# Loading w by sets of rows and x's first chunks by channel halves, with eight output slots started side by side

## The chip, the cores and the metric

The kernel runs on one core of one Trainium2 chip. The metric is the device time in microseconds (us). Three runs of the kernel before gave a median of 903.98 us (903.84 to 904.01).

## The reference

A batch of sequences is multiplied by a square matrix, and the product is summed along the sequence with one decay for each output channel:

```python
B, S, D = (16, 2048, 1024)
xw = x @ w
out[:, 0, :] = xw[:, 0, :]
for t in range(1, S):
    out[:, t, :] = decay[None, :] * out[:, t - 1, :] + xw[:, t, :]
```

All of x (128 MB), w (4 MB) and the output (128 MB) are float32. The kernel multiplies in bf16 and accumulates in float32.

## The kernel before

**Chunks and slots.** The 32,768 rows of x are cut into 64 chunks of 512 rows (`TL`), four to a sequence, and the chunks are taken in pairs, `groups`. The 1024 output channels are eight slots `n` of 128 channels, made of 32 from each quarter of the channels. A step of the main loop is one slot of one pair of chunks, so a tile has 128 partitions (channels) and 1024 columns (time); the last two chunks are handled singly. The product of a slot and a chunk takes eight matrix products `k` (`K` = 8), each with 128 input channels and 512 columns, summed in one PSUM bank.

**From x to a product.** `load` (letter L, or M for the first two chunks) brings a chunk from DRAM to `xb` in four DMAs, one for each 32 partitions, on GpSimd's queue, casting to bf16 on the way. `turn` (letters T and E, line 115) transposes blocks of 32 by 32 on VectorE. It treats two bf16 channels as one 32-bit word, so that `xw` holds two neighbouring channels beside each other. `part` (letters X, Y, F, G, line 123) copies `xw` to `xt` and pulls the two channels apart. `matmul` (line 131) reads its columns either from `xt`, where they stand close, or from `xw` with a gap between them (`pairs`).

**w.** It is loaded once by `load_w` into the tiles that later hold outputs (`stage`), in four sets (h, e): h is the half of the columns, e the parity of the rows. The first set goes by SP's and ACT's queues as float32, the other three by GpSimd's queue (letter U) with a cast. `settle` (letters W, w, q, Q; lines 330 and 379) copies a set into `wsb` in the order that the products need.

**From a product to the output.** A tile is scanned along time on VectorE in one of two ways. A tile that isn't `paired` is scanned straight from PSUM (letter S, line 233). For a paired tile ACT copies the bank to `xs` (p, line 186) and scales the even columns (g, line 169), GpSimd joins them into the odd columns (j, line 208), VectorE scans half as many columns with the squared decay (S, line 213), and ACT and GpSimd fill the even columns in again (h, line 169, and c, line 266). `keep` (k, z) carries the last column to the next tile of the slot. VectorE transposes the result back (B, line 283) and SP stores it. A set `flips` of step numbers says which tiles take the other way than the rule by slot.

**PSUM.** There are eight banks: three double tiles `ps`, in turn, and two single ones, `spare` and `spare1`. A bank can be written again when ACT or VectorE has read it. `spare1` also holds the squared decays from the letter d on.

**The order of work.** Each engine works through its own instructions in the order in which the program writes them. This order is written out by hand for the start and the end, in `agenda`: a string of letters for each step, performed after the step's products have been written; step -99 stands for all before the first product. In between it follows a rule (`usual`), into which the turns and copies of later chunks are put by `later`. At most eight of GpSimd's DMAs are under way; the ninth is issued when the first has landed.

**The start.** TensorE first multiplies zeros (`spin`), and then goes on with gate tiles, one for each quarter of the first load (`spin_on`, letter K), so that these products wait for the load. Step 0 then works on four slots in two parts: the first chunk by halves of its rows, the even `k` first, in four banks; then the second chunk in four other banks. Steps 4 to 7 follow with two banks each, and step 8 interleaves two slots of the second pair of chunks.

Of the kernel before, what the change touches and what calls it, by code (L numbers as in the profile page):

```python
# [9 lines left out]
FP32 = mybir.dt.float32  # L10
# [15 lines left out]
def kernel(  # L26
# [82 lines left out]

    def turn(c, j0=0, j1=NJ, m0=0, m1=M):  # L110
        if c not in xw_of:
            xw_of[c] = ring(sb, "xw", 2, [128, M, NJ, P, 2], BF16)
        src = xb_of[c][:, j0:j1].rearrange("p j c -> p (j c)").bitcast(FP32)
        dst = xw_of[c].rearrange("p m j i e -> p (m j i e)").bitcast(FP32)
        pin(nc.vector.transpose(  # L115
            out=dst.rearrange("p (m j i) -> p j m i", m=M, i=P)[:, j0:j1, m0:m1],
            in_=src.rearrange("p (j m c) -> p j m c", m=M, c=P)[:, :, m0:m1]))
# [172 lines left out]
    class Outlet:  # L290
# [8 lines left out]
        def store(self, b, t0, j0, j1):  # L299
# [4 lines left out]
            for j in range(j0, j1, nj):  # L304
# [10 lines left out]
    size = M * CH  # L315
    stage = {(0, 0): room[0][:, 0:size],
             (0, 1): room[0][:, size:size * 3 // 2].bitcast(BF16),
             (1, 0): room[1][:, 0:size // 2].bitcast(BF16),
             (1, 1): room[1][:, size // 2:size].bitcast(BF16)}

    def load_w(queues, h, e):
        for i, q in enumerate((0, 2, 1, 3)):
            pin(queues[i % len(queues)].dma_start(  # L323
                out=stage[h, e][quad(q)].rearrange("p (m d) -> p m d", m=M),
                in_=_ap(w, [[2 * D, P], [2 * P * D, M], [1, CH]],
                        (q * CQ + e) * D + h * CH)))

    def settle(h, e, m, copy):
        src = stage[h, e][:, m * CH:(m + 1) * CH]
# [7 lines left out]
    load_w((nc.sync, nc.scalar), 0, 0)  # L337
# [21 lines left out]
    def load_half(i):  # L359
        for q in range(NQ):  # L360
            load(i // 2, q, *halves[i % 2])

    def spin_on(q):
        pin(nc.scalar.copy(out=gates[q][quad(q), 0:1], in_=xb_of[0][quad(q), 0, 0:1]))
        spin(3 if q < NQ - 1 else 2, gates[q])

    def load_part(i):
        load_w((nc.gpsimd,), *((0, 1), (1, 0), (1, 1))[i])
# [3 lines left out]

    def settle_one(i, copy):
        settle(i // 8, i // 4 % 2, i % 4, copy)

    def settle_slots(i, r0, r1):
        h, e, m = i // 8, i // 4 % 2, i % 4
        src = stage[h, e][:, m * CH:(m + 1) * CH]
        pin(nc.vector.tensor_copy(  # L379
            out=wcols[:, 2 * m + e, h, :, r0:r1],  # L380
            in_=src.rearrange("p (q r i) -> p q r i", q=NQ, r=R)[:, :, r0:r1]))
# [91 lines left out]
    slots = [(g, n) for g in groups[:-1] for n in range(K)]  # L473
# [3 lines left out]
    def turn_and_load(c):  # L477
# [15 lines left out]
        "W": lambda i: settle_one(i, nc.vector.tensor_copy),  # L493
        "w": lambda i: settle_one(i, nc.scalar.copy),
        "M": load_half,
        "U": load_part,
# [4 lines left out]
        "q": lambda i: settle_slots(i, 0, 1),  # L501
        "Q": lambda i: settle_slots(i, 1, R),
# [22 lines left out]
        -99: "M0 M1 U0 M2 M3 U1 U2 w0 W1 w2 W3 K0 K1 K2 K3 E0 E1 G0 E2 G1 E3 F2 G3 E4 E5 G4 E6 G5 E7 F6 G7 q4 w5 Q4 W6 W7 D E8 E9 G8 E10 G9 E11 F10 G11 E12 L E13 G12 L E14 G13 E15 L F14 G15",  # L525
        0: "p0 z0 W8 W9 W10 W11",
        1: "g0",
        2: "L S1 L",
        3: "p2 z2 L g2 j0 S3 w12 w13 L w14 L w15 k1",
        4: "j2 B1 d k3",  # L530
        5: "p4 L S0 L g4 S2 L k0 h0 j4 B3 h2",
        6: "k2 c0 T2 c2 p5 g5 B0 L X2 L",
        7: "B2 L L Y2 T3 L z4 z5 j5 p6 S4 z6 L g6 L X3 S5 j6 S7 Y3 L S6 h4 k7 k5 c4 k4 h5 B7",
        8: "",
        9: "k6 h6 c5 B4",
        10: "p8 g8 c6 T4 z8 p9 j8 g9 B5 X4",
        11: "L j9 B6 p10 S8 L z9 z10 g10 S9 h8",
        12: "j10 Y4 S11 L c8 h9 T5 c9",
        13: "p12 L g12 B9 j12 X5 S10 L",
        14: "Y5 B8 L B11 h10 z12 c10 S13",  # L540
        15: "p14 L g14 S12 j14 T6 h12 L",
# [186 lines left out]
```

## Time and profile before

| | |
|---|---|
| median of three runs | 903.98 us |
| profiled execution, its own device time | 903.68 us |
| its span, from first to last instruction | 901.9 us |
| TensorE busy | 892.0 us (99%) |
| VectorE, ACT, GpSimd busy | 825.6, 687.6, 657.0 us |
| granted TensorE clock | 1.00 throughout |
| read from and written to DRAM | 138.4 and 134.2 MB |

The span is one execution; 1.8 us of its device time lie outside it. A busy share is an average over the whole span. Products are pipelined: a product's length in the table (0.38 us) is longer than the time from one start to the next, so the pace is read from starts. An instruction's line is that of the helper that wrote it, and an engine's idle time in square brackets names what ended it.

### The profile page before, as it was taken

Reading aid. Unit: us, or ns where it says so; the run is one execution under the profiler, and the core shown is the slowest. Engines: PE = TensorE matmul, PEld = TensorE weight load, DVE = VectorE, ACT = ScalarE, POOL = GpSimd, SP = SyncE. Lnnn points to the kernel's source line nnn. Section 1 sums busy time; section 2 is a strip of 40 time slices with the busy share of each in tenths; the row PEclk is TensorE's granted clock in tenths of the full one; section 3 lists DMA queues with packets and bytes.
Section 4 is the critical chain, followed back from the end, with each engine's and each line's share of the span. In section 5 each row is a group of like instructions: output and inputs, shape, how many; then the busy total and the mean of one; then the engine's idle time right before and its main releaser. Section 6 shows DMA issues by size and latency. Waiting matters only on the chain.

```text
span 901.9 us, 12226 instructions
## 1 busy us (share of the span) xinstructions
PE 892.0 (99%) x4127; PEld 412.1 (46%) x4209; DVE 825.6 (92%) x636; ACT 687.6 (76%) x962; POOL 657.0 (73%) x755
## 2 busy tenths in 40 slices
PE   9999999999999999999999999999999999999998
PEld 5544444444444444444444444444444444444444
DVE  4999999999999999999998999999999999999998
ACT  4889867777877877878778778777787787787743
POOL 7888678777767768777677687777777777776532
PEclk9999999999999999999999999999999999999999
DMA  9999999999999999999999999999999999999768
GB/s 193 196 215 217 231 218 217 215 240 253 254 249 252 248 249 252 242 247 230 225 234 228 224 228 228 233 228 228 232 229 228 227 230 225 228 226 222 176 152 234
DMA packets 403182, 204.77 MB, mean 227 GB/s; under 512 B 9392, under 2 KB 402096, under 8 KB 403120
## 3 DMA queue, kind: packets, MB, share of 16 engines
q1 hardware_dynamic: 265808, 134.77, 60.9%
q0 software_dynamic: 137024, 68.70, 56.7%
q8 instruction: 33, 0.54, 0.2%
q10 hardware_dynamic: 288, 0.52, 0.2%
q14 instruction: 29, 0.24, 0.1%
HBM read 138.42 MB, written 134.22 MB: 302 GB/s over the span
## 4 chain that ended last, share of the span: by engine, by line
PE 97%; DMA 1%; issue 1%; POOL 0%; DVE 0%; ACT 0%; DVEq 0%; POOLq 0%
PE ps L131 96%; PE spare L131 1%; DMA xb<-in_x_dram 1%; DMA ot<-in_w_dram 1%; POOL ot L323 0%; DVE so L233 0%; PE ps L419 0%; PE spare L419 0%; ACT xb L426 0%; DVE wsb L379 0%; DVEq L379 0%; POOLq L712 0%
## 5 line engine op out<-in xcount | busy, mean ns | idle before, releaser
L131 PE MATMUL ps<-xt,wsb 128*128 128x512 bf16 x3934 | 860.8, 378 | 4.7 <-DVE wsb L379 0.4
L131 PEld LDWEIGHTS <-wsb 128*128 128x128 bf16 x4160 | 406.8, 98 | 478.7 <-ACT wsb L330 0.8
L208 POOL TENSOR_TENSOR xs<-h,xs 128x512 f32<-128x512 f32 (+1 forms) x190 | 243.0, 1279 | 189.8 <-ACT h L169 84.6
L186 ACT COPY xs<-ps 128x1024 f32<-128x1024 f32 (+1 forms) x190 | 188.9, 994 | 156.9 <-PE ps L131 146.3
L283 DVE STREAM_TRANSPOSE ot<-so 128x1024 f32<-128x1024 f32 (+2 forms) x265 | 300.4, 1172 | 2.5 <-POOL so L202 1.1
L266 POOL TENSOR_TENSOR so<-h,xs 128x512 f32<-128x512 f32 (+1 forms) x190 | 241.5, 1273 | 41.2 <-ACT h L169 27.0
L123 ACT COPY xt<-xw 128x2048 bf16<-128x2048 bf16 (+1 forms) x136 | 242.3, 1790 | 7.6 <-DVE xw L115 7.4
L105 POOL DMA_DIRECT2D xb<-in_x_dram x264 | 174.3, 661 | 3.0 <-POOLq L712 0.9
L169 ACT ACTIVATE h<-so,dec 128x512 f32<-128x512 f32 (+1 forms) x190 | 145.4, 766 | 25.5 <-DVE so L213 22.3
L115 DVE STREAM_TRANSPOSE xw<-xb 128x2048 f32<-128x2048 f32 (+1 forms) x78 | 147.3, 1900 | 5.3 <-DMA xb<-in_x_dram 5.3
L213 DVE TENSOR_TENSOR_SCAN so<-spare,keep,xs 128x512 f32<-128x512 f32 (+1 forms) x97 | 120.0, 1240 | 27.6 <-POOL xs L208 27.2
L213 DVE TENSOR_TENSOR_SCAN so<-spare,xs 128x512 f32<-128x512 f32 x93 | 113.3, 1220 | 27.2 <-POOL xs L208 24.4
L169 ACT ACTIVATE h<-ps,dec 128x512 f32<-128x512 f32 (+1 forms) x189 | 129.5, 685 | 0.0
L233 DVE TENSOR_TENSOR_SCAN so<-dec,ps 128x1024 f32<-128x1024 f32 x34 | 76.9, 2261 | 0.8 <-ACT h L169 0.6
L233 DVE TENSOR_TENSOR_SCAN so<-dec,keep,ps 128x1024 f32<-128x1024 f32 (+2 forms) x35 | 74.8, 2140 | 0.0
L270 ACT COPY keep<-so 128x1 f32<-128x1 f32 x136 | 25.4, 189 | 9.1 <-DVE so L233 8.6
L204 ACT COPY so<-keep 128x1 f32<-128x1 f32 x97 | 18.4, 191 | 2.4 <-DVE ot L283 2.2
L131 PE MATMUL spare<-xt,wsb 128*128 128x512 bf16 (+1 forms) x64 | 12.9, 332 | 0.0
L131 PE MATMUL ps<-xw,wsb 128*128 128x256 bf16 (+1 forms) x68 | 11.2, 301 | 0.0
L202 POOL MEMSET so<- 128x1 f32 x93 | 10.7, 117 | 0.6 <-DVE ot L283 0.6
L323 POOL DMA_DIRECT2D ot<-in_w_dram x12 | 6.5, 546 | 3.2 <-DMA xb<-in_x_dram 1.9
L348 PE MATMUL spare<-idle 128*128 128x512 bf16 x22 | 6.8, 483 | 1.2 <-DVE idle L338 1.2
(40 smaller groups left out, 40.5 us busy)
## 6 DMA issues: line engine op xcount, KB each, us to landing
out_dram<-ot SPq DMA_DIRECT2D x236, 512.0 KB, 10.8
xb<-in_x_dram POOLq DMA_DIRECT2D x248, 256.0 KB, 7.8
out_dram<-ot SPq DMA_DIRECT2D x56, 128.0 KB, 2.6
xb<-in_x_dram POOLq DMA_DIRECT2D x16, 128.0 KB, 5.7
out_dram<-ot SPq DMA_DIRECT2D x8, 256.0 KB, 4.5
ot<-in_w_dram POOLq DMA_DIRECT2D x12, 128.0 KB, 5.1
out_dram<-xb SPq DMA_DIRECT2D x4, 256.0 KB
ot<-in_w_dram ACTq DMA_DIRECT2D x2, 256.0 KB, 5.1
```

The source lines that it names most:

```text
L105: pin(nc.gpsimd.dma_start(out=xb_of[c][quad(q), j0:j1], in_=_ap(x, [[D, P], [P * D, j1 - j0], [1, CQ]], (b * S + t0 + j0 * P) * D + q * CQ)))
L115: pin(nc.vector.transpose(out=dst.rearrange("p (m j i) -> p j m i", m=M, i=P)[:, j0:j1, m0:m1], in_=src.rearrange("p (j m c) -> p j m c", ...
L123: pin(copy(out=xt_of[c][:, m0:m1, :, j0 * P:j1 * P], in_=src))
L131: pin(nc.tensor.matmul(out=ps[:, t0:t1] if ps.shape[1] >= t1 else ps, lhsT=lhs, rhs=rhs, start=(k == 0 and t0 == start), stop=(k == K - 1),))
L169: pin(nc.scalar.activation(out=h, in_=src, func=mybir.ActivationFunctionType.Copy, scale=dec[:, self.n:self.n + 1]))
L186: pin(nc.scalar.copy(out=self.xs[:, i * size:(i + 1) * size], in_=ps))
L208: pin(nc.gpsimd.tensor_tensor(out=odds, in0=self.g, in1=odds, op=ALU.add))
L213: pin(nc.vector.tensor_tensor_scan(out=so[:, 3:T + 2:2], data0=squares[-1][:, n:n + 1].to_broadcast([128, T // 2]), data1=self.xs[:, 1:T:2 ...
L233: pin(nc.vector.tensor_tensor_scan(out=so[:, t + 2:t + 2 + size], data0=dec[:, n:n + 1].to_broadcast([128, size]), data1=ps, initial=befor ...
L266: pin(nc.gpsimd.tensor_tensor(out=self.so[:, 2:T + 2:2], in0=self.h, in1=self.xs[:, 0:T:2], op=ALU.add))
L270: pin(nc.scalar.copy(out=self.keep, in_=self.so[:, self.T + 1:self.T + 2]))
L283: pin(nc.vector.transpose(out=outlet.ot[:, j:j + size, c0:c0 + P], in_=self.so[:, t1:t1 + size * P].rearrange("p (i t) -> p i t", t=P)))
```

## The change

Only the start is changed, up to step 41 of the new numbering.

- The first pair of chunks is no longer taken together: chunk 0 and chunk 1 are sixteen steps of 512 columns each, and later steps have numbers higher by eight.
- w comes in four sets `m` of 256 rows with all 1024 columns (64 rows from each quarter of the channels, each two neighbouring ones on one partition), so that a DMA moves 32 pieces of 8 KB instead of 128 pieces of 2 KB. Set m serves the products k = 2m and 2m + 1 of all eight slots.
- Chunks 0 and 1 are loaded by `load_side` in halves of channels (128 of each quarter's 256): five loads M0 to M4, of which M0, M3 and M4 are half a chunk and M1 and M2 a quarter. A piece is 512 B in DRAM and 256 B as written. `turn` has a branch for this layout.
- The queue on GpSimd becomes M0 U1 M1 U2 M2 U3 M3 M4.
- Step 0 writes the products of all eight slots for chunk 0 into all eight banks, in the order of k. The products k = 0, 1, 4, 5 are taken by halves of the rows and read `xw`; the others read `xt`.
- Chunk 1's products all read `xw`. Its first four slots (step 8) run side by side, then come four more, each to its end.
- The gate spins are 3, 2, 2 and 1 instead of 3, 3, 3 and 2.
- The agenda and the flips for the first 41 steps are new.

The diff, cut to its core:

```diff
+    def load_side(c, q, side, j0, j1):
+        ...
+        wide = CQ // 2
+        dst = xb_of[c].rearrange("p j c -> p (j c)").rearrange(
+            "p (g j c) -> p g j c", g=2, c=wide)
+        pin(nc.gpsimd.dma_start(
+            out=dst[quad(q), side, j0:j1],
+            in_=_ap(x, [[D, P], [P * D, j1 - j0], [1, wide]],
+                    (b * S + t0 + j0 * P) * D + q * CQ + side * wide)))
...
-                out=stage[h, e][quad(q)].rearrange("p (m d) -> p m d", m=M),
-                in_=_ap(w, [[2 * D, P], [2 * P * D, M], [1, CH]],
-                        (q * CQ + e) * D + h * CH)))
+                out=stage[m][quad(q)],
+                in_=_ap(w, [[2 * D, P], [1, 2 * D]], (q * CQ + 2 * m * P) * D)))
...
     def load_half(i):
+        c, side, j0, j1 = ((0, 0, 0, NJ), (0, 1, 0, H), (0, 1, H, NJ),
+                           (1, 0, 0, NJ), (1, 1, 0, NJ))[i]
         for q in range(NQ):
-            load(i // 2, q, *halves[i % 2])
+            load_side(c, q, side, j0, j1)
...
-        spin(3 if q < NQ - 1 else 2, gates[q])
+        spin((3, 2, 2, 1)[q], gates[q])
...
-    slots = [(g, n) for g in groups[:-1] for n in range(K)]
+    slots = [([c], n) for c in groups[0] for n in range(K)]
+    slots += [(g, n) for g in groups[1:-1] for n in range(K)]
...
-        -99: "M0 M1 U0 M2 M3 U1 U2 w0 W1 w2 W3 K0 K1 K2 K3 E0 E1 G0 E2 G1 E3 F2 G3 E4 E5 G4 E6 G5 E7 F6 G7 q4 w5 Q4 W6 W7 D E8 E9 G8 E10 G9 E11 F10 G11 E12 L E13 G12 L E14 G13 E15 L F14 G15",
+        -99: "M0 U1 M1 U2 M2 U3 M3 M4 w1 W0 w3 W2 K0 K1 K2 K3 E0 E4 E1 E5 G1 G5 W4 W5 W6 w7 E2 E3 G3 D W8 W9 W10 w11 E6 E7 G7 W12 W13 W14 w15",
+        7: "z3 z2 L S1 L L p3 E12 k1 p2 L S0 g3 L g2 p4 E8 j2 E9 k0 E13 S2 E15 E10 E14 j3 S3 E11",
+        11: "g4 j4 k2 h2 L c2 k3 h3 B0 L p5 B1 c3 g5 S4 j5 p6 B3 k4 z4 g6 z5 L S5 h4 j6 B2 k5 h5 T2 c4",
+        13: "z6 c5 p7 g7 z7 L p10 j7 S6 X2 B5 L S7 L S9",
+        14: "g10 L k6 h7 j10 h6 B4 k9 c7 Y2 B9",
+        15: "c6 S8 L p11 L S13 T3 p14 g11 g14",
...
-    flips = (1, 13, 15, -19, -18, -11, -8, -6, -3, -2)
+    flips = (0, 1, 3, 7, 8, 9, 11, 12, 13, 16, 19, 21, 23, 27, 35, 37, 38, -19, -18, -11, -8, -6, -3, -2)
...
+            both = [ring(psp, "ps", 3, [128, 2 * TL]) for _ in range(3)]
+            heads = [ps[:, i * TL:(i + 1) * TL] for ps in both for i in range(2)] + spares
             for k0 in range(0, K, 2):
+                if k0 in (0, M):
+                    for j0, j1 in halves:
+                        for k in (k0, k0 + 1):
+                            for i in range(K):
+                                matmul(heads[i], i, k, xt_of.get(0), j0 * P, j1 * P,
+                                       pairs=xw_of[0])
+                elif k0 < M:
+                    for k in (k0, k0 + 1):
+                        for i in range(K):
+                            matmul(heads[i], i, k, xt_of[0])
+                else:
+                    for i in range(K):
+                        for k in (k0, k0 + 1):
+                            matmul(heads[i], i, k, xt_of[0])
...
+        elif step == K:
+            both = [ring(psp, "ps", 3, [128, 2 * TL]) for _ in range(2)]
+            ...
+            for i0 in range(0, R, 2):
+                for k in range(M):
+                    for i in range(i0, i0 + 2):
+                        matmul(heads[i], i, k, xt_of.get(1), pairs=xw_of[1])
             for i in range(R):
+                for k in range(M, K):
+                    matmul(heads[i], i, k, xt_of.get(1), pairs=xw_of[1])
```

## The prediction

> **What bounds the kernel now.** I read the page's busy lines first, then what TensorE waited for, then the timelines of TensorE and VectorE over the first 50 us, where the change lies.
>
> The page's busy line and TensorE's waits over the whole span:
>
> ```profile
> PE 892.0 (99%) x4127; PEld 412.1 (46%) x4209; DVE 825.6 (92%) x636; ACT 687.6 (76%) x962; POOL 657.0 (73%) x755
> ...
> PE spare L348 <- DVE idle L338: 1.2, 1, 1.2
> PE spare L348 <- ACT gate L364: 0.4, 1, 0.4
> PE ps L131 <- DVE wsb L379: 0.4, 1, 0.4
> ```
>
> TensorE is the bound, and it waits for almost nothing. Whatever the change does reaches the end only through the start of the first real product, the pace of a product, and new waits of TensorE. Its timeline (start, length, operation):
>
> ```profile
> 8.45 2.55 PE L348 MATMUL spare<-idle,gate 128*128 128x512 bf16 x11 [0.44 <-ACT gate L364]
> 10.83 0.50 PE L131 MATMUL ps<-xw,wsb 128*128 128x256 bf16 x3
> ...
> 15.04 0.82 PE L131 MATMUL ps<-xt,wsb 128*128 128x512 bf16 x2 [0.36 <-DVE wsb L379]
> ...
> 41.20 1.89 PE L131 MATMUL spare<-xt,wsb 128*128 128x512 bf16 x8
> 42.93 3.79 PE L131 MATMUL ps<-xw,wsb 128*128 128x512 bf16 x16
> 46.55 3.61 PE L131 MATMUL ps<-xt,wsb 128*128 128x512 bf16 x15
> ```
>
> Real work starts at 10.83, right behind the eleven gate spins. Eight products from xt take 42.93 - 41.20 = 1.73 us, so 0.216 each; sixteen from xw, whose rows are read with a gap, take 46.55 - 42.93 = 3.62 us, so 0.226. A 256-wide product from xw takes 0.113 (10.83 to 12.53: 15 starts in 1.70). The sixteen xt products before 42.93 are slot 8's first, so chunks 0 and 1 end at 42.93 - 16 x 0.216 = 39.48. That is the mark to beat: with everything behind it unchanged, the change is worth its shift of this mark.
>
> VectorE's timeline shows when the load sets arrive, as each first instruction waits for one:
>
> ```profile
> 9.58 1.42 DVE L115 STREAM_TRANSPOSE xw<-xb 128x256 f32<-128x256 f32 x4 [1.62 <-DMA xb<-in_x_dram]
> 12.21 1.43 DVE L115 STREAM_TRANSPOSE xw<-xb 128x256 f32<-128x256 f32 x4 [0.89 <-DMA xb<-in_x_dram]
> 14.79 0.36 DVE L379 COPY wsb<-ot 128x128 bf16<-128x128 bf16 x2 [0.85 <-DMA ot<-in_w_dram]
> 17.53 1.42 DVE L115 STREAM_TRANSPOSE xw<-xb 128x256 f32<-128x256 f32 x4 [1.35 <-DMA xb<-in_x_dram]
> 20.23 1.42 DVE L115 STREAM_TRANSPOSE xw<-xb 128x256 f32<-128x256 f32 x4 [0.96 <-DMA xb<-in_x_dram]
> ...
> 26.76 1.19 DVE L233 TENSOR_TENSOR_SCAN so<-dec,spare 128x512 f32<-128x512 f32 x1
> ```
>
> The loads arrive in a stream without gaps: M0 at 9.58, M1 at 12.21, U0 at 14.79, M2 at 17.53, M3 at 20.23. An x set (four DMAs, 1024 packets of 512 B, 0.5 MB as written) takes 2.63, 2.74, 2.70, mean 2.69 us; the w set (512 packets of 1 KB, as many bytes) 2.58. The two rows give a price: 0.11 us for 512 packets more, and 2.47 us for the bytes.
>
> **The change, part by part.**
>
> *Loads.* The order on POOL's queue becomes M0 U1 M1 U2 M2 U3 M3 M4. A row of x is cut in two, so a set M0, M3 or M4 has 2048 packets of 256 B: 2.47 + 4 x 0.11 = 2.91 us. M1 and M2 are half sets of 1024: 1.46. A w set has 128 packets of 4 KB: 2.50. No row shows x packets under 512 B. The lower bound is the price by bytes alone (2.69); the upper is a packet that costs as much as one of 512 B (5.38, and 2.69 for M1, M2). I take 2.91, on the line through the two rows and near the lower end, because halving the packets there changed the time by only 4%. What waits for a set can then start: M0 9.58 + 0.22 = 9.80, U1 12.30, M1 13.76, U2 16.26, M2 17.72, U3 20.22, M3 23.13, M4 26.04. POOL issues a 512-packet DMA in 0.66 us against the 0.73 that it moves in, and eight DMAs may be under way, so issuing keeps ahead; M1 and M2 issue at 0.58 each against 0.36, but their turn to issue comes when M0 lands (about 8 us) and they move from 12.3 on. The first w set on SP and ACT has longer rows; I cost that at nothing, as the casts that need it (7.16 and 7.20) have over 2 us until M0.
>
> The Trainium skill (DMA: Bandwidth & Descriptors, Specifications) says that line rate needs transfers of at least 512 B and that below it the engine does a read-modify-write. That speaks against this change; no trace here shows it, and by it the time would be that of the first rival below.
>
> *First product.* The gates keep the spins until M0's last quarter has landed; there are 8 instead of 11. Gate copy (0.19) after 9.76, one spin (0.22), the turn of the first tile 9.80 + 0.36: the first product starts at 10.25 instead of 10.83. Gain 0.6.
>
> *Slots 0 to 7 of chunk 0, in eight banks.* Channels 0-1 by halves: 32 x 0.113 = 3.63, to 13.88. Channels 2-3: U1 at 12.30 and three copies of 0.29 are done by 13.2, so 16 x 0.216 = 3.45 runs at once, to 17.33. Channels 4-5: U2 16.26, its first copy 16.6 and third 17.15; M2's first turn 18.1, needed at 19.14; 3.63, to 20.96. Channels 6-7: U3 20.22, copies at 20.5, 20.8 and 21.1; the third is needed at 21.18; 3.45, to 24.41. No wait, but the last margin is 0.1.
>
> *The step to chunk 1.* Its first product needs the turns E8 and E12 and the bank pair ps0, which scans S1 and S0 empty; VectorE's order is S1, E12, S0, E8. Slot 1 ends at 20.96 + 3 x 0.216 + 0.38 = 22.0. S1 (1.19, the row above) ends at 23.2, just when M3 is there (23.13); E12 0.36, S0 1.15, E8 0.36: 25.1. TensorE would have come at 24.41, so here is a new wait of 0.7. Queued behind E8 are the turns E9 and E13, which products 0.45 us later need and get.
>
> *Chunk 1's 64 products* read xw: 64 x 0.226 = 14.5 against 13.8 from xt. That costs 0.7. The 256-wide xw products stay 64; 32 from xt (0.109 each) go, worth 0.04. The two waits of before in this stretch (0.36, and about 0.2 not listed but seen as gaps in starts) go.
>
> Sum: 25.15 + 14.5 = 39.65 against 39.48, so +0.2.
>
> *What is late next.* Slot 16 needs ps0 again, emptied by S9 and S8. VectorE's order from E8 on, by row means (256 transposes 0.36, half scans 0.73, 512 turns back 0.62 as half of 1.22, T2 2.27, 512 scans 1.2): E9 E13 S2 E15 E10 E14 S3 E11, 28.7; B1 B0 S4 B3 S5 B2, 32.7; T2, 34.9; S6 B5 S7 S9 B4 B9, 39.4; S8, 40.6. Back to back, each starts some 0.07 earlier than the row before ends (24.57 + 2.27 against 26.76), which takes 1.5 off: 39.1. Slot 16 wants it at 39.65. So a wait of 0 to 0.9; I take 0.3. T3 for chunk 3 (by 42.5 to 44) is wanted at 43.1 plus that wait: nothing.
>
> *Load on the engines.* Eight whole tiles become sixteen half ones. By counts and row means: VectorE 16 transposes of 0.68 for 8 of 1.22, 9 half scans of 0.73 and net 5 of 1.25 for 5 of 1.25 and 2 of 2.3, fewer copies: +2 us. ACT -2, POOL +0.3. VectorE works without a gap from 25 to 110 us (10.00 of 10.00 in the stretch 100 to 110) and has 16.52 of 20.00 after 120. The 2 us are thus absorbed there, if the banks come free in time meanwhile; cost 0, upper bound 2. The end part is as it was.
>
> Total: -0.6 + 0.7 + 0.7 - 0.6 (waits gone) + 0.3 = +0.5 us. On the profiled run (901.9 span, 1.8 outside it, 903.68) that is 904.2; the median is 0.3 higher, so 904.5.
>
> **Rivals.**
>
> 1. *Small packets cost more.* If a 256-B packet took as long as one of 512 B, the sets come at M0 12.3, U1 14.8, M1 17.5, U2 20.0, M2 22.7, U3 25.2, M3 30.6, M4 35.9; E12, S0 and E8 let chunk 1 start at 32.5, it stops at 36.1 until M4's turns at 37.0 and ends at 37.0 + 48 x 0.226 = 47.9: +8.4, 912.4. Halfway (4.03 a set) M3 comes at 26.5, chunk 1 starts at 28.5 and ends at 43.0: +3.5, 907.5. It decides from a set price of about 3.5, where M3 is 1.5 us late and S0 and E8 still stand behind it. For: no row. Against: the small effect from 1 KB to 512 B. Chance 0.19, most of it nearer the half.
>
> 2. *VectorE's queue gives the banks back late.* S0 before E8, S8 at slot 16, T3, and the margin of 0.1 at U3 all sit on one engine that is full until 110 us. If the row means held without overlap (0.9 at slot 16) and the 2 us of added work showed as bank waits before 110, it is +0.2 + 0.9 + 1 to 2: 906.1 to 907.1. For: the 10.00s. Against: before lives with the same fullness and TensorE waits for none of it. Chance 0.17.
>
> 3. *The head start is larger.* If w's long rows free the engines sooner and M0 lands 0.7 earlier, everything up to S1 moves: first product 9.5, chunk 1 at 24.4: -0.5, 903.5; with no wait at chunk 1 nor slot 16, 902.7. Below that it can't go, since the xw pace keeps its 0.7. This rival is no change by the measure; over 0.2% gain needs still more. Chance 0.12, of which 0.04 for faster.
>
> **How the numbers follow.** The forecast case has 0.52. 0.2% is 1.8 us, about what a measurement of this kernel can tell from no change: same is 902.2 to 905.8. Forecast and most of rival 3 fall in it: 0.60. Rivals 1 and 2 lie above: 0.36. The range goes from rival 3's middle (903.1) to halfway in rival 1 (907.5), leaving out some 0.06 below and 0.12 above.
>
> **What would show it.** First real product near 10.25; E12 at 23.2 and chunk 1's first product near 25.1 with a wait of 0.7 on VectorE; 0.226 a product through chunk 1; slot 16 at 39.7 to 40.5. Rival 1 shows as E0 later than 10.5 and waits for DMA before channels 4-5; rival 2 as waits for VectorE or ACT between 39 and 110. A first product before 9.5 or TensorE waits beyond 1.5 us in total would make the prediction wrong.

## The result and the profile after

The changed kernel is slower: 912.68 us (median of four, 912.39 to 913.18) against 903.91 us for the kernel before in the same runs (903.55 to 904.01), a ratio of 1.0098 with a 95% interval of 1.0081 to 1.0116. The profiled span is 910.8 us against 901.9. The forecast was 904.5 and no change.

First the page's busy line and TensorE's waits of the changed kernel, which answer to the same views of before.

```profile
PE 897.3 (99%) x4190; PEld 409.9 (45%) x4190; DVE 831.4 (91%) x648; ACT 684.2 (75%) x974; POOL 660.0 (72%) x769
...
PE ps L152 <- DVE xw L130: 2.3, 2, 1.6
PE ps L152 <- DVE so L254: 2.2, 2, 1.3
PE ps L152 <- ACT h L190: 1.6, 1, 1.6
...
PE ps L152 <- DVE wsb L351: 1.2, 2, 0.9
```

The busy line still says 99%, because a busy share is an average and a waiting product's length is modelled. The waits say more: before, products waited 0.4 us in all after the gate; now they wait 7.3 us, and a VectorE instruction ends most of it. TensorE's timeline shows the places:

```profile
11.03 0.84 PE L152 MATMUL ps<-xw,wsb 128*128 128x256 bf16 x6
...
22.82 0.39 PE L152 MATMUL ps<-xt,wsb 128*128 128x512 bf16 x1 [0.92 <-DVE wsb L351]
...
28.44 4.40 PE L152 MATMUL ps<-xw,wsb 128*128 128x512 bf16 x18 [1.58 <-DVE xw L130]
33.59 6.91 PE L152 MATMUL ps<-xw,wsb 128*128 128x512 bf16 x30 [0.75 <-DVE xw L130]
...
45.43 1.25 PE L152 MATMUL ps<-xt,wsb 128*128 128x512 bf16 x5 [1.33 <-DVE so L254]
...
71.66 65.79 PE L152 MATMUL ps<-xt,wsb 128*128 128x512 bf16 x304 [1.65 <-ACT h L190]
138.33 1.89 PE L152 MATMUL ps<-xt,wsb 128*128 128x512 bf16 x8 [0.88 <-DVE so L254]
```

The first product starts at 11.03 instead of 10.83. Slot 16's first product, for which the prediction set the mark of 39.48, starts at 45.43. The last product starts at 906.92 instead of 898.02, 8.90 later. Taken as the distance of two starts less the pace, the parts are: first product +0.2; U3's copies 1.1 and 0.4; chunk 1's start 1.7; the turn E11 0.9; slot 16 1.5; a bank behind ACT's `h` at 71.7 1.8; a bank behind a scan at 138.3 1.0; the pace of chunk 1 from xw 0.7; less the 0.6 of waits that before had. The sum is 8.7, which leaves 0.2 in small gaps.

VectorE's timeline shows when the loads came, and what the early scans took:

```profile
7.96 0.76 DVE L351 CAST wsb<-ot 128x512 bf16<-128x512 f32 x2 [6.45 <-DMA ot<-in_w_dram]
10.53 1.42 DVE L130 STREAM_TRANSPOSE xw<-xb 128x256 f32<-128x256 f32 x4 [1.81 <-DMA xb<-in_x_dram]
12.61 0.86 DVE L351 COPY wsb<-ot 128x512 bf16<-128x512 bf16 x3 [0.65 <-DMA ot<-in_w_dram]
...
17.36 0.74 DVE L351 COPY wsb<-ot 128x512 bf16<-128x512 bf16 x3 [2.00 <-DMA ot<-in_w_dram]
18.94 0.77 DVE L130 STREAM_TRANSPOSE xw<-xb 128x256 f32<-128x256 f32 x2 [0.84 <-DMA xb<-in_x_dram]
22.47 0.92 DVE L351 COPY wsb<-ot 128x512 bf16<-128x512 bf16 x3 [2.76 <-DMA ot<-in_w_dram]
...
26.50 0.45 DVE L130 STREAM_TRANSPOSE xw<-xb 128x256 f32<-128x256 f32 x1 [0.97 <-DMA xb<-in_x_dram]
...
29.28 1.91 DVE L234 TENSOR_TENSOR_SCAN so<-squares,xs 128x256 f32<-128x256 f32 x1 [0.25 <-POOL xs L229]
```

M0's first turn came at 10.53 (the sum said 9.80), M1's at 14.05 (13.76), U2's copy at 17.36 (16.26), U3's at 22.47 (20.22), M3's turn at 26.50 (23.13). The stream of loads, which the sum took as unbroken, is 0.7 late at M0 and 0.3 at M1, and then falls behind: by 1.1 at U2, 2.2 at U3 and 3.4 at M3.

At the end of the run-up there is one more line to see, T11, the turn of chunk 11, the last chunk loaded there:

```profile
121.85 1.25 DVE L234 TENSOR_TENSOR_SCAN so<-spare,keep,xs 128x512 f32<-128x512 f32 x1
124.71 2.31 DVE L136 STREAM_TRANSPOSE xw<-xb 128x2048 f32<-128x2048 f32 x1 [1.62 <-DMA xb<-in_x_dram]
```

VectorE stands still for 1.6 us until chunk 11 has landed (124.6); it is the only gap of 0.1 us or more that VectorE has from 70 us up to there. Before, chunk 11 landed at 110.9 and was turned at 113.5 without a wait.

### The profile page after: what moved, and what is told of

The parts are those of the page before. It is cut to its first block, busy times and chain, and to the rows that moved or that the text cites. A ratio compares the mean times of both kernels' runs of the same rounds, so it can differ in the third digit from the quotient of the medians.

```text
span 910.8 us, 12335 instructions
## 1 busy us (share of the span) xinstructions
PE 897.3 (99%) x4190; PEld 409.9 (45%) x4190; DVE 831.4 (91%) x648; ACT 684.2 (75%) x974; POOL 660.0 (72%) x769
## 4 chain that ended last, share of the span: by engine, by line
PE 84%; DVE 3%; POOL 2%; issue 2%; DMA 1%; ACT 1%; DVEq 0%; POOLq 0%; ACTq 0%
PE ps L152 83%; DMA xb<-in_x_dram 1%; DVE so L234 1%; DVE so L254 1%; DVE ot L304 1%; POOL so L287 1%; POOL xs L229 1%; PE spare L152 1%; POOL xb L105 1%; ACT h L190 0%; ACT xs L207 0%; ACT so L225 0%; PE ps L429 0%; PE spare L429 0%; ACT keep L291 0%
## 5 line engine op out<-in xcount | busy, mean ns | idle before, releaser
L152 PE MATMUL ps<-xt,wsb 128*128 128x512 bf16 x3944 | 851.6, 379 | 5.0 <-DVE so L254 2.2
L144 ACT COPY xt<-xw 128x2048 bf16<-128x2048 bf16 (+1 forms) x128 | 238.9, 1867 | 6.7 <-DVE xw L130 4.3
L105 POOL DMA_DIRECT2D xb<-in_x_dram x248 | 164.3, 663 | 3.4 <-DVE xw L136 1.5
L136 DVE STREAM_TRANSPOSE xw<-xb 128x2048 f32<-128x2048 f32 x62 | 141.6, 2284 | 1.6 <-DMA xb<-in_x_dram 1.6
L234 DVE TENSOR_TENSOR_SCAN so<-spare,keep,xs 128x512 f32<-128x512 f32 (+1 forms) x93 | 115.1, 1239 | 27.9 <-POOL xs L229 27.6
L234 DVE TENSOR_TENSOR_SCAN so<-spare,xs 128x512 f32<-128x512 f32 x89 | 108.5, 1220 | 26.5 <-POOL xs L229 23.8
L254 DVE TENSOR_TENSOR_SCAN so<-dec,keep,ps 128x1024 f32<-128x1024 f32 (+2 forms) x40 | 81.9, 2051 | 0.0
L254 DVE TENSOR_TENSOR_SCAN so<-dec,ps 128x1024 f32<-128x1024 f32 (+1 forms) x33 | 72.5, 2197 | 1.7 <-PE ps L152 0.9
L152 PE MATMUL ps<-xw,wsb 128*128 128x512 bf16 (+1 forms) x112 | 21.8, 339 | 2.3 <-DVE xw L130 2.3
L117 POOL DMA_DIRECT2D xb<-in_x_dram x20 | 12.4, 628 | 4.1 <-DMA xb<-in_x_dram 3.1
L130 DVE STREAM_TRANSPOSE xw<-xb 128x256 f32<-128x256 f32 x16 | 6.0, 414 | 4.2 <-DMA xb<-in_x_dram 4.2
```

The lines of the kernel that those rows point to most:

```text
L105: pin(nc.gpsimd.dma_start(out=xb_of[c][quad(q), j0:j1], in_=_ap(x, [[D, P], [P * D, j1 - j0], [1, CQ]], (b * S + t0 + j0 * P) * D + q * CQ)))
L136: pin(nc.vector.transpose(out=dst.rearrange("p (m j i) -> p j m i", m=M, i=P)[:, j0:j1, m0:m1], in_=src.rearrange("p (j m c) -> p j m c", ...
L144: pin(copy(out=xt_of[c][:, m0:m1, :, j0 * P:j1 * P], in_=src))
L152: pin(nc.tensor.matmul(out=ps[:, t0:t1] if ps.shape[1] >= t1 else ps, lhsT=lhs, rhs=rhs, start=(k == 0 and t0 == start), stop=(k == K - 1),))
L234: pin(nc.vector.tensor_tensor_scan(out=so[:, 3:T + 2:2], data0=squares[-1][:, n:n + 1].to_broadcast([128, T // 2]), data1=self.xs[:, 1:T:2 ...
L254: pin(nc.vector.tensor_tensor_scan(out=so[:, t + 2:t + 2 + size], data0=dec[:, n:n + 1].to_broadcast([128, size]), data1=ps, initial=befor ...
```

## The experiments

Ratios are to the kernel before in the same runs. The changed kernel's 912.7 is the figure to compare the medians with, and its ratio of 1.0098.

**Rows of w and small packets.** Is it the 4-KB packets of w, or the 256-B packets of x, that make the loads late? w's first set was loaded in pieces of 2 KB, written 16 columns apart so that they stay pieces (`w0_pieces`), and then all four sets (`w_pieces`):

```diff
-                in_=_ap(w, [[2 * D, P], [1, 2 * D]], (q * CQ + 2 * m * P) * D)))
+                in_=_ap(w, [[2 * D, P], [CH, 4], [1, CH]], (q * CQ + 2 * m * P) * D)))
```

> The changed kernel with one edit: the first set of w, on the queues of SP and ACT, moves as 128 pieces of 2 KB a DMA (as in the kernel before) instead of 32 rows of 8 KB; the pieces of a row lie 16 elements apart in the staging tile where needed. Theory A (the long rows on the two hardware queues hold up the first x load): the casts of w start at 7.2 instead of 7.96, the first turn at 9.7 instead of 10.53, the first product at 10.4 instead of 11.03; later sets hang on the issues of GpSimd, which begin again when the first quarter of M0 lands (8.5 to 7.8), so they too come up to 0.7 earlier: 912.0 or a little under. Theory B (M0 is late because of its own 256-B packets): casts at 7.2, but the first turn stays at 10.3 or later and the time at 912.7.

> As the run before, but all four sets of w move as pieces of 2 KB (1 KB as written). Theory A (packets of 4 KB as written make U2 and U3 late, as a DMA then has only two packets on each of 16 engines): the copies of U2 start at 16.3 instead of 17.36 and of U3 at 20.5 instead of 22.47, and the time falls below the run before by some 1.5 us. Theory B (the queue runs dry, because eight DMAs may be under way and M1 and M2 fill four places each with half the bytes): U2 and U3 come when they came in the run before, within 0.4.

Measured: 914.83 us, ratio 1.0122 [1.0107, 1.0137], and 913.94 us, ratio 1.0109 [1.0093, 1.0126]. Short pieces are no help; they make the start worse, and the cast at 7.2 that both theories expected did not come. VectorE's first lines of `w0_pieces`:

```profile
9.23 0.76 DVE L355 CAST wsb<-ot 128x512 bf16<-128x512 f32 x2 [7.71 <-DMA ot<-in_w_dram]
11.90 1.42 DVE L130 STREAM_TRANSPOSE xw<-xb 128x256 f32<-128x256 f32 x4 [1.91 <-DMA xb<-in_x_dram]
```

The first x packet moved at 3.99 instead of 5.66, while w's first set was moving (its last packet ended at 7.92 instead of 6.49), and both landed later: the cast at 9.23 against 7.96, M0's turn at 11.90 against 10.53. That the two loads hold each other up fits this, but no run separates it from the shorter pieces, and why x began earlier is not shown. Behind the start nothing changed: in `w_pieces` U2 came at 18.39 and U3 at 24.43, within 0.4 us of those of `w0_pieces` (18.22 and 24.84). w's 4-KB packets are not what makes U3 late. Nor are the 256-B packets of x dearer than summed: 512 of them, one quarter of a set, start within 0.75 to 0.76 us in the middle of M0 and within 0.73 to 0.75 in M3 and M4, and the prediction's line through two rows gave 2.91 / 4 = 0.73.

**One load in place of two.** M1 and M2 together are one half of the channels. In `m1_whole` M1 brings it whole and M2 is dropped, so the order on the queue is M0 U1 M1 U2 U3 M3 M4, with as many bytes and packets but four DMAs fewer:

```diff
-        c, side, j0, j1 = ((0, 0, 0, NJ), (0, 1, 0, H), (0, 1, H, NJ),
+        c, side, j0, j1 = ((0, 0, 0, NJ), (0, 1, 0, NJ), None,
```

> The changed kernel with one edit: M1 brings the whole second half of channels of chunk 0 in four DMAs and M2 is left away, so the order is M0 U1 M1 U2 U3 M3 M4 with 28 DMAs instead of 32. Same bytes, same packets. If the small DMAs starve the queue (eight under way, half the bytes in each): the copies of U3 start at 21.3 or earlier instead of 22.47, E12 (M3) at 25.3 instead of 26.5, and the time falls by 1 to 1.5 us, to some 911.4. If packets of 4 KB are to blame: U3 and M3 as in the changed kernel, 912.7. By the sum of the prediction, which saw no starving, nothing changes either.

Measured: 910.28 us, ratio 1.0072 [1.0057, 1.0087], 2.4 us less. U3's copies start at 20.33 where the sum had said 20.22, chunk 0 has no wait left, and chunk 1 starts 1.8 us earlier. In the traces the gain is 1.9 at slot 16 (43.57 against 45.43), and 0.8 more at the wait for `h` (1.0 against 1.8). This second part is not the edit's: the wait for `h` is 1.0 in `w0_pieces` too. The DMA view between 12 and 22 us gives the reason; the first line is of the changed kernel, the second of `m1_whole`:

```profile
DMA packets 2746, 1.64 MB, mean 164 GB/s; under 512 B 2489, under 2 KB 2489, under 8 KB 2745
```

```profile
DMA packets 3938, 1.95 MB, mean 195 GB/s; under 512 B 3681, under 2 KB 3681, under 8 KB 3937
```

With more small packets in the same time, `m1_whole` moves 1.95 MB and the changed kernel 1.64 (the kernel before 1.96). GpSimd's timeline of the changed kernel shows the issues:

```profile
8.79 0.59 POOL L117 DMA_DIRECT2D xb<-in_x_dram  x1 [2.80 <-DMA xb<-in_x_dram]
9.67 1.71 POOL L117 DMA_DIRECT2D xb<-in_x_dram  x3 [0.29 <-DMA xb<-in_x_dram]
11.37 1.98 POOL L344 DMA_DIRECT2D ot<-in_w_dram  x4
13.33 2.31 POOL L117 DMA_DIRECT2D xb<-in_x_dram  x4
15.62 1.03 POOL L344 DMA_DIRECT2D ot<-in_w_dram  x2
16.88 1.12 POOL L344 DMA_DIRECT2D ot<-in_w_dram  x2 [0.23 <-DMA ot<-in_w_dram]
```

M0 and U1 hold the eight places, so M1's first issue waits until 8.79, and there is no stock ahead. From there GpSimd issues with one pause of 0.29 us: M1, U2 and M2 (the four at 13.33), until U3's first at 15.62. These twelve DMAs bring 0.26 + 0.52 + 0.26 MB in 6.83 us, 153 GB/s, against the 196 that the stream of before moved at between 12 and 22 us. A DMA of a half load takes 0.58 us to issue and one of a whole load, in `m1_whole`, 0.65, for twice the bytes. At U3's third DMA (16.88) GpSimd waits for a place again, and M2 holds four of the eight with half the bytes. `m1_whole` takes both away, so it doesn't tell the issuing time from the places.

There is one more cost in M3. In `m1_whole` U3 is on time, but M3's turn E12 comes at 24.68, 1.5 later than summed. Near it the DMA view has one packet of another kind; this is the changed kernel between 20 and 22 us:

```profile
q8 instruction: 1, 0.02, 3.0%
```

This packet has 16 KB. In `m1_whole` it starts at 21.68 and takes 1.00 us. The trace has 16 landing records for each DMA: for M3's last quarter 15 of them had come by 23.55, and the last came at 24.56. In `early_whole`, an experiment below with the same start, the packet begins only at 22.62; there all 16 are in by 23.39, and chunk 1's wait is 0.7 instead of 1.35. So some 1.0 us of M3's lateness goes with this packet. That it holds up one share of each load is an inference, since the trace doesn't name the engines.

**The price of the early scans.** The changed kernel copies the squared decays to PSUM only at 74 us (letter d at step 23, since `spare1` holds outputs until then); before it is done at 29. Until then a paired tile's scan reads both inputs from SBUF. `before_sbuf_squares` is the kernel before without d; `before_late_d` has d at step 17 instead of 4, and ran twice:

```diff
-        4: "j2 B1 d k3",
+        4: "j2 B1 k3",
...
-        17: "z14 Y6 S14 L B13 z15 h14 S15 p16 z16 c14",
+        17: "d z14 Y6 S14 L B13 z15 h14 S15 p16 z16 c14",
```

> The kernel before without letter d: the squared decays stay in SBUF for the whole run and are not copied to PSUM. Theory (a scan that reads both of its inputs from SBUF is slowed while GpSimd works, which is why half scans took 1.06 us instead of 0.73 and 512 scans 1.82 instead of 1.28 in the changed kernel): the 183 paired scans of 512 columns take 1.6 to 1.8 instead of 1.25, 60 to 100 us more on VectorE, which becomes the bound: 930 to 960 us. Rival (the slow scans are a matter of the crowded start alone): the mean stays under 1.35 and the time within 2 us of 903.9.

> The kernel before with letter d (the copy of the squared decays to PSUM) moved from step 4 to step 17, so that it runs near 72 us, as late as in the changed kernel (74 us); nothing else. Theory (squares in SBUF slow the paired scans, and that is what makes VectorE give banks back late between 30 and 75 us in the changed kernel): 512 scans before 72 us take 1.7 instead of 1.25, some 12 of them, 5 to 6 us more on VectorE in a stretch where it has no idle time; TensorE gets new waits for VectorE or ACT of 2 to 4 us in total, 906 to 908. Rival (the late banks come from the load times and the new order): scans longer, but TensorE waits under 0.6 us and the time is within 0.6 us of 903.7.

> The kernel before with the squared decays copied to PSUM at step 17 instead of step 4, once more, because the profiled execution of the first run took 904.0 us and showed no late scans' waits, while its six timed executions took 908. Theory (scans with both inputs in SBUF are slow only while GpSimd works beside them, so their cost depends on how the two engines fall together): a profiled execution of 908 shows scans so<-squares,xs at 1.4 us or more and bank waits of 3 to 4 us in sum between 40 and 110 us. Rival (the 908 executions are slowed by something else, for instance a lower clock): their traces show no such waits.

Measured: `before_sbuf_squares` 919.51 us, ratio 1.0169 [1.0154, 1.0184]; the expected time was too high, as VectorE had 76 us of slack to take the load. Its groups of scans, with those of the kernel before under them:

```profile
L213 DVE TENSOR_TENSOR_SCAN so<-squares,xs 128x512 f32<-128x512 f32 x93 | 160.7, 1732 | 1.3 <-POOL xs L208 1.3
L213 DVE TENSOR_TENSOR_SCAN so<-squares,keep,xs 128x512 f32<-128x512 f32 x90 | 147.6, 1640 | 1.7 <-POOL xs L208 1.1
```

```profile
L213 DVE TENSOR_TENSOR_SCAN so<-spare,keep,xs 128x512 f32<-128x512 f32 x90 | 115.0, 1280 | 27.6 <-POOL xs L208 27.2
L213 DVE TENSOR_TENSOR_SCAN so<-spare,xs 128x512 f32<-128x512 f32 x93 | 113.3, 1220 | 27.2 <-POOL xs L208 24.4
```

The same scan takes 1.73 us instead of 1.22 when the factors lie in SBUF, and 1.64 instead of 1.28 where it goes on from an earlier tile (`keep`). The price depends on GpSimd. Of the 183 scans of a whole tile in that run, the 60 with under 0.3 of their time beside a GpSimd addition took 1.21 us on average, the 118 with 0.3 to 0.9 of it 1.94 and up to 3.83, and five with more 1.46. With the factors in PSUM no such scan of the kernel before took over 1.29, though 108 of its 183 ran beside additions for over 0.9 of their time. The Trainium skill (SBUF — State Buffer, Who interferes with whom) says that a VectorE instruction with two SBUF inputs contends with a GpSimd instruction that reads SBUF, and that the second to start stands still until the first has ended. The trace mostly agrees, for this scan, which the page does not name: the 113 scans that began while an addition ran took what was left of the addition and 1.11 us more on average, and of the 39 in which the first addition began later, 36 took 1.21. The other three took 2.85 to 3.83, which the rule does not explain.

`before_late_d` gave 907.98 us (ratio 1.0044 [1.0032, 1.0056]), as expected; one of its seven executions, the profiled one, took 903.96, and its scans of a whole tile from SBUF took 1.35 us on average. The second run gave 907.86 (1.0048 [1.0032, 1.0064]). Its trace, of an execution of 908.15 us, has 1.82 for the same nine scans, among them these:

```profile
30.30 4.93 DVE L213 TENSOR_TENSOR_SCAN so<-squares,xs 128x512 f32<-128x512 f32 x2
...
42.93 4.09 DVE L213 TENSOR_TENSOR_SCAN so<-squares,xs 128x512 f32<-128x512 f32 x2
```

Of each pair the first took 1.18 us, the second 3.83 and 2.98. Beside the first of these two GpSimd adds without a break from 31.60 to 34.13, and 1.18 + 2.53 is 3.71, nearly the whole of it, though the scan is recorded as begun 0.2 us before the addition. TensorE then waits 1.8 us for ACT's xt and 1.5 for scans. So a few early scans moved the whole kernel by 4 us in nine executions and by nothing in one; that it depends on how the engines fall together is the likely reason.

**Order of VectorE's work.** `whole_s0` is `m1_whole` with S0 put ahead of E12; `tuned` has in addition E11 ahead of S3, and S9 B4 S8 ahead of S7.

```diff
-        7: "z3 z2 L S1 L L p3 E12 k1 p2 L S0 g3 L g2 p4 E8 j2 E9 k0 E13 S2 E15 E10 E14 j3 S3 E11",
+        7: "z3 z2 L S1 L L p3 S0 k1 p2 L E12 g3 L g2 p4 E8 j2 E9 k0 E13 S2 E15 E10 E14 j3 S3 E11",
```

> The run with M1 as one load, with one more edit: VectorE scans S0 before the turn E12 instead of behind it (S1 S0 E12 E8). In that run E12 waits for M3 until 24.68 and S0 and E8 stand behind it; chunk 1 starts at 26.62. If the order is what makes a late M3 cost so much, S0 ends at 25.2, E12 and E8 follow to 25.9 and chunk 1 starts at 26.0: 0.6 us less, 909.7. If later waits take over, the waits at E11 and at slot 16 grow by what is gained here: 910.3.

> The run before, with two more turns of the order on VectorE: E11 before S3, and S9 B4 S8 before S7 in steps 13 to 15 instead of S7 S9 B4 B9 S8. Theory (each remaining wait up to 46 us is the place of one instruction in VectorE's queue): the wait for E11 (0.9) goes and the one at slot 16 (1.5) falls to 0.3 or less, 2 us less than the run before: 907.7. Rival (VectorE has too much to do for any order, with squares in SBUF): the waits move on to the stretch 46 to 140 us and the time stays within 0.8 us of the run before.

Measured: 910.76 us, ratio 1.0081 [1.0066, 1.0096], and 913.40 us, 1.0107 [1.0090, 1.0124]. In `whole_s0` the wait at chunk 1's start falls from 1.35 to 0.66, and others come in its place (0.65 at 30.4, 0.9 at 132.1). In `tuned` the wait for E11 moves to another turn (1.15 at 30.6), slot 16 still waits 1.5, and a new one comes, because h7 and Y2 stand behind the later S7:

```profile
42.99 1.04 PE L152 MATMUL ps<-xt,wsb 128*128 128x512 bf16 x4 [1.34 <-DVE so L254]
46.43 1.86 PE L152 MATMUL ps<-xt,wsb 128*128 128x512 bf16 x4 [2.40 <-ACT xt L144]
```

ACT stands still for 3.48 us before h7 there. The waits move from place to place, and neither order wins anything, so the theory that these orders were the fault is not borne out. The rival isn't either: the time of `tuned` is 2.6 us above `whole_s0`, and between 25 and 70 us VectorE itself stands still for 1.1 us in `whole_s0` and 2.2 in `tuned`, against 0.5 in `m1_whole`. Whether some other order would win is open.

**Scans at the predicted price.** `priced_scans` is the changed kernel, `priced_whole` is `m1_whole`, with the scans before d cut to 96 of 256 and 256 of 512 columns:

```diff
+                size = T // 2 if len(squares) > 1 else {256: 96, 512: 256}[T // 2]
+                if size < T // 2:
+                    pin(nc.vector.memset(so[:, 3 + 2 * size:T + 2:2], 0.0))
                 pin(nc.vector.tensor_tensor_scan(
-                    out=so[:, 3:T + 2:2],
+                    out=so[:, 3:2 + 2 * size:2],
...
```

> The changed kernel in which VectorE's scans of paired tiles cost, until the squared decays are copied to PSUM, about what the prediction priced: of 256 columns only 96 are scanned and the rest set to zero, of 512 only 256 (their output columns are therefore not the reference's). Aimed at 0.73 us for the pair of instructions of a half tile and 1.25 us for a whole one, against 1.06-1.09 and 1.82 measured. Theory A (the later waits are the dear scans on VectorE): 12 scans cost 4.8 us less; chunk 0's waits (1.1 and 0.4 at U3's copies) stay, chunk 1's start waits as before within 0.2 (S0 and S1 there are scanned from PSUM), the wait for E11 at 33.6 shrinks from 0.9 to 0.2 or less, slot 16 from 1.5 to 0.3 or less, those at 71.7 (1.8) and 138.3 (1.0) vanish: 907.5 to 908.5. Rival B (it is the order of VectorE's work and the late loads; a shorter scan only lets VectorE idle elsewhere): the waits at slot 16 and later keep more than half of their length, 910.5 or more.

> Both repairs: the early scans cut as above (left-out columns are set to zero), and chunk 0's second half of channels loaded by one load M1 of 512-B DRAM pieces for all its rows instead of M1 and M2. If the two terms named so far (loads that come late because small loads use up the eight places under way, and scans dearer than priced) are the whole of what the prediction missed and add up: 910.3 (one load) less 4 to 4.5 us of waits (E11 0.9, slot 16 1.5, the h wait 1.0, the scan wait 1.0) = 905.8 to 906.3, near the forecast of 904.5, the rest being M0's later arrival and M3's. Rival: a third cost is hidden behind these waits; then it stays over 907.5.

Measured: 910.66 us, ratio 1.0077 [1.0062, 1.0092], and 909.18 us, 1.0060 [1.0043, 1.0077]. The twelve cut scans with their fills took 9.8 us in `priced_scans`, against 15.0 in the changed kernel and 10.3 at the prediction's prices. The waits at which the theory aimed went: in `priced_scans` those for E11 and for `h` vanish and slot 16's falls from 1.5 to 0.3. Yet only 2.0 and 1.1 us were won, so both times lie where the rivals had them. Part was given away in `priced_scans` at the start, where U3's first copy cost 2.7 instead of 1.1: the 16-KB packet came at 21.77, and of the 16 landing records of U3's last quarter 15 had come by 22.37 and the last at 23.87. The rest came back later. `priced_whole`:

```profile
125.87 3.61 PE L152 MATMUL ps<-xt,wsb 128*128 128x512 bf16 x16 [0.74 <-DVE so L257]
130.41 3.61 PE L152 MATMUL ps<-xt,wsb 128*128 128x512 bf16 x16 [0.92 <-DVE so L257]
134.90 5.34 PE L152 MATMUL ps<-xt,wsb 128*128 128x512 bf16 x23 [0.88 <-DVE so L257]
```

There the scans stand behind T11, and T11 waits for chunk 11, 3.85 us in `priced_scans` and 4.19 here. In all eight traces of changed kernels up to here T11 starts within 0.2 us of chunk 11's landing, after a wait of 1.5 to 4.2. Set side by side, they have one constant (differences from unrounded starts):

| kernel | T11 starts | last product starts | difference |
|---|---|---|---|
| changed | 124.71 | 906.92 | 782.21 |
| w0_pieces | 126.52 | 908.73 | 782.21 |
| w_pieces | 126.07 | 908.28 | 782.21 |
| m1_whole | 121.94 | 904.15 | 782.21 |
| whole_s0 | 122.99 | 905.19 | 782.21 |
| tuned | 125.42 | 907.63 | 782.21 |
| priced_scans | 122.53 | 904.74 | 782.21 |
| priced_whole | 121.27 | 903.48 | 782.21 |

From T11 on everything is rigid in these eight: whatever happened before it, the last product starts 782.21 us after T11. The constant says that the way to the end leads through T11; it does not say what T11 waits for.

**Without chunk 11's load.** `no_chunk11_load` is the changed kernel, `priced_no_chunk11` is `priced_whole`, with T11 turning chunk 10's data:

```diff
+        if c == 11:
+            xb_of[c] = xb_of[10]
+            return
```

> The changed kernel without the load of chunk 11: T11 turns chunk 10's data instead, so the output rows of chunk 11 are not the reference's. In eight traces of changed kernels so far the last product starts 782.21 us after T11 starts, and T11 starts when the last quarter of chunk 11 has landed (after: 124.6). Theory C (the landing of chunk 11 sets the end): without it T11 starts right behind the scan before it, at 123.1 instead of 124.7, the wait at 138.3 (1.0) vanishes and the time falls by 1.0, to 911.5 to 912.0; the fixed distance of 782.2 is gone. Rival (VectorE's order alone sets that wait): 912.5 or more, with the wait at 138.3 still there.

> priced_whole (scans cut short, one load M1) without the load of chunk 11, as above. Theory C: T11 starts at 117.1 to 118.6 instead of 121.3, the three waits at 125.9, 130.4 and 134.9 (0.9, 1.1, 1.0) vanish, and the time falls from 909.2 to 906.0 to 906.8: the two terms named earlier (late loads, dear scans) then show their full worth, which the landing of chunk 11 had hidden. Rival (the waits there belong to VectorE's order): 908.5 or more.

Measured: 910.42 us, ratio 1.0078 [1.0063, 1.0093], and 906.45 us, 1.0031 [1.0019, 1.0043]. The first won 2.3 where 1.0 was expected. In its trace the wait at 138 (1.0) is gone; besides, slot 16 starts 0.4 earlier and the wait for `h` is 0.8 shorter. These two lie before 71 us, and chunk 11's load was issued only from 103 us on in the changed kernel, so they are not chunk 11's doing, and what made them is not shown. The second is within the expected band. T11 starts at 121.73 and 117.51, and the distance to the last product is 782.89 and 783.28. TensorE's waits in the second:

```profile
PE ps L155 <- DVE xw L133: 1.4, 1, 1.4
PE spare L375 <- DVE idle L365: 1.2, 1, 1.2
PE spare L375 <- ACT gate L393: 0.9, 1, 0.9
PE spare L155 <- ACT h L193: 0.2, 1, 0.2
```

After the gate only 1.6 us are left. With M1 in one load, the scans near the price of the sum and chunk 11 out of the way, 6.2 of the 8.8 us are gone (912.68 to 906.45); what stays is the wait at chunk 1's start (1.5), the pace of chunk 1 (0.7) and a few tenths.

**Earlier loads.** Why is chunk 11 late? Chunk 9 is loaded into the buffer that T6 frees, and T6 comes at 86.0 (before: 67.3); no load is under way from 80.2 to 90.1, while stores move 2.4 MB. `early_turns` (on the changed kernel) and `early_whole` (on `m1_whole`) move T6 from step 27 to 25, T7 from 28 to 27, and four loads into step 26:

```diff
-        25: "p23 S22 g23 z25 B19 h22 j23 p24 B20 c22 z23 g24",
-        26: "S23 j24 p25 B22 h23 z24 S24 z26 g25 c23",
-        27: "T6 k24 h24 j25 p26 c24 g26 S25 X6 j26",
+        25: "p23 S22 T6 g23 z25 B19 h22 j23 p24 B20 c22 z23 g24",
+        26: "S23 L j24 L p25 B22 h23 L z24 S24 L z26 g25 c23",
+        27: "T7 k24 h24 j25 p26 c24 g26 S25 X6 j26",
```

> The changed kernel with T6 moved from step 27 to step 25, T7 from step 28 to T6's old place, and four load letters L into step 26, so that chunk 9's load is issued some 8 us earlier (it reuses the buffer that T6 frees; after: T6 at 86.0, issues at 90.1 to 96.0). Theory C1 (chunk 11's landing is late because the queue of loads stood empty between 80.2, when chunk 8 had landed, and 90.1, while only stores moved): chunk 11 lands 4 to 8 us earlier, T11 no longer waits for it, the wait at 138.3 vanishes; cost: the scans behind T6 come 2.3 us later, 0 to 1.5 in new bank waits between 76 and 95; 911.5 to 913. Theory C2 (the engines are full in any order, so chunk 11 lands when its bytes and those of the stores have moved): it lands less than 2 us earlier, 912.5 or more.

> The same moves in m1_whole (910.3; its T11 waits until 121.9 and TensorE then 1.0 at 135.6). Theory C1: that wait vanishes, 909.3, plus 0 to 1.5 of new bank waits. Theory C2: 910 or more.

Measured: 912.42 us, ratio 1.0096 [1.0081, 1.0112], and 911.38 us, 1.0087 [1.0070, 1.0104]. Chunk 11 lands at 117.7 instead of 124.6 in the first: its lateness was one of order, as C1 said. But nothing is won, and `early_whole` is 1.1 slower than `m1_whole`. `early_turns` on VectorE:

```profile
94.14 1.25 DVE L304 STREAM_TRANSPOSE ot<-so 128x1024 f32<-128x1024 f32 x1 [0.26 <-POOL so L287]
97.30 1.23 DVE L234 TENSOR_TENSOR_SCAN so<-spare,xs 128x512 f32<-128x512 f32 x1 [1.91 <-POOL so L223]
...
124.24 2.29 DVE L136 STREAM_TRANSPOSE xw<-xb 128x2048 f32<-128x2048 f32 x1
```

T11 waits for no load now, and still starts at 124.24, only 0.5 earlier. VectorE lost the time on the way. With the turns moved ahead it has gaps of 2.3 us between 91 and 98, most of them in front of the scan at 97.30, which waits until GpSimd has set up its tile; GpSimd adds and issues loads without a gap from 85.7 to 97.3. In `no_chunk11_load`, with the turns in their old places and no load to wait for, VectorE has no such gap, and T11 starts at 121.73. TensorE also waits for ACT's xt (1.1 in all). From T11 to the last product it is 782.2 us again in both runs, without a wait for a load. So the edit put a wait for GpSimd in the place of the one for chunk 11, and does not show what an earlier load alone is worth.

## Why the prediction was wrong, step by step

**Right.** The price of a 256-B packet (0.73 a quarter set, measured 0.73 to 0.76), the pace of chunk 1 (0.7), the two old waits that go (0.6), and the order in which E12, S0 and E8 release chunk 1. Rival 1 named 912.4, nearly what came, but for a cause that the spacing of 0.74 us refutes: the number was met by chance. The Trainium skill (DMA: Bandwidth & Descriptors, Specifications) says that line rate needs transfers of at least 512 B. The trace agrees in the direction, with an extra of 0.06 to 0.09 us for a quarter set over the price by bytes (0.67), and not in the size that rival 1 gave it.

**"M0 at 9.80, first product at 10.25" was 0.8 off, the term of -0.6 being +0.2.** The step that failed is "I cost that at nothing" for w's first set. That set came later too: its cast at 7.96 instead of 7.20. M0's first packet moved at 5.66 instead of 5.14, and from its first packet's start to its last's M0 took 3.67 us instead of 3.21, where the sum had allowed 0.22 more for the small packets; its turn came at 10.53. In `w0_pieces`, where x moved earlier beside that set, both landed 1.3 to 1.4 us later. This fits two loads that hold each other up; why M0's first packet came later is not shown.

**"Issuing keeps ahead" is the step that failed first behind M0.** It noted that M1 and M2 issue more slowly than they move (0.58 against 0.36), and excused it with a head start that isn't there: the places are counted in DMAs, M1 can't be issued before M0 lands, and a half load then fills four places with half the bytes. `m1_whole` takes that away and puts U3 where the sum had it; it is worth 1.9 us at slot 16, of the 2.4 by which its time fell.

**"M3 23.13" and the "new wait of 0.7" at chunk 1's start.** The sum let M3 follow U3 by 2.91. In `m1_whole`, with U3 on time, it follows by 4.35 (20.33 to 24.68), and the wait is 1.35. Some 1.0 of that goes with the 16-KB packet, for which the sum had no term: in `early_whole`, where it came too late for M3, the wait is 0.7, as summed.

**The half scan "0.73" and "the 2 us are absorbed; cost 0" are the next failure.** The row of 0.73 was taken with the factors in PSUM. In the changed kernel they lie in SBUF until 74 us: 1.06 to 1.09 for a half tile, 1.82 for a whole one, 4.8 us over twelve scans. The diff showed the letter d moving from step 4 to 23, and the trace of before had no row for such a scan beside GpSimd; it should have been bounded like the packets. It falls on an engine that in the changed kernel has no gap of 0.1 us or more from 30 to 123 us, so it came out as waits of 0.9, 1.5 and 1.8 (1.0 in seven other traces) at 33.6, 45.4 and 71.7, which `priced_scans` all but removes. That is rival 2's mechanism, at one and a half times its price or more (4.2 against 1.9 to 2.9). The sum for slot 16 also took a turn back of 512 columns at 0.62, while the sum of VectorE's load had 0.68 for it; 0.68 was measured, some 0.4 us over the seven turns in that sum.

**"With everything behind it unchanged" is the last.** The sum stopped at slot 16. Behind it, T6 had moved from 67 to 86 us, and with it chunk 9's and chunk 11's loads, and no line of the sum looked at them. `no_chunk11_load` and `priced_no_chunk11` show that this load is a limit of its own, some 1.0 us in the changed kernel and 2.7 behind the other repairs, and that it hides what those win. `early_turns` lands it earlier and wins nothing, because that order makes VectorE wait for GpSimd.

What stays open: the worth of each cause alone, since the three limits lie so close together that each repair uncovers the next; whether issuing time or the eight places made the loads late; and why the first execution of `before_late_d` was spared.

## What to carry to other kernels

When several engines are full, a start-up that wins bytes or waits in one place must be followed to the point where the slowest of the other queues has slack again (here 140 us, not 40), and a removed wait is only worth the distance to the next limit. Look for a constant distance between one event and the end over several variants: it names a place through which the way to the end leads, where a list of waits does not; what holds that place needs a run of its own. An operand that moves from PSUM to SBUF is a change of price, and small DMAs use up issuing time, and places in a queue that counts DMAs and not bytes. An edit that moves work of a full engine can make that engine wait elsewhere, so look at its gaps before you call it the limit.

## What the runs showed of the hardware

- A scan of 512 columns whose factors and data are both in SBUF took 1.21 us on average with a GpSimd addition beside it for under 0.3 of its time, and up to 3.83 with more (`before_sbuf_squares`); with the factors in PSUM it never took over 1.29 in the kernel before.
- 512 packets of 256 B as written took 0.73 to 0.76 us, and the same bytes in 256 packets of 512 B 0.67 us (2.69 a set): halving a packet cost some 10%.
- With an earlier first packet of x (3.99 instead of 5.66) and w in shorter pieces, the load of w beside it landed 1.3 us later, and M0 itself 1.4 us later (`w0_pieces`).
- One 16-KB packet of the kind "instruction" moved for 0.94 to 1.10 us at 20.6 to 22.6 us in every trace of a changed kernel; in `m1_whole` the last of the 16 landing records of the load behind it came 1.01 us after the fifteenth.
